# Two chunks of the FFN in one pass for a single tile, and fewer paired passes in layer 0

## The chip, the cores and the metric

The kernel runs on 1 core of one Trainium2 chip. The metric is the device time of one execution in microseconds (us), the median of several runs. The engines of the core work side by side, each on its own queue of instructions, and wait for each other through semaphores: PE (TensorE) multiplies matrices, DVE (VectorE) and ACT (ScalarE) work element by element, SP issues most of the DMAs. PE runs at a clock that a throttle grants; the profile shows the granted share, 1.00 being full speed.

## The reference

A two-layer encoder step on 1024 prompt rows and 32 sample rows, all float32. What matters here is the channel MLP (FFN) at the end of each layer, and the norms around it:

```python
for i in range(DEPTH):                       # DEPTH = 2
    mod = jax.nn.silu(c) @ w_ada[i] + b_ada[i]
    sh1, sc1, gt1, sh2, sc2, gt2 = jnp.split(mod[:, None, :], N_MOD, axis=-1)
    h = rmsnorm(x, g_norm[i, 0]) * (1 + sc1) + sh1
    ...                                      # layer 0: gating mixer, layer 1: pooling mixer
    x = x + gt1 * rmsnorm(mix, g_norm[i, 1])
    h = rmsnorm(x, g_norm[i, 2]) * (1 + sc2) + sh2
    f = jnp.square(jax.nn.relu(h @ ffn_w_up[i])) @ ffn_w_down[i]   # 1024 -> 4096 -> 1024
    x = x + gt2 * rmsnorm(f, g_norm[i, 3])
```

## The kernel before

**Tiles.** The rows are cut into three tiles of columns: tiles 0 and 1 have 384, tile 2 has 288 (256 prompt rows and the 32 sample rows). Activations lie with channels on the 128 partitions. Every float32 product is made of three matmuls in the reduced format fp32r: each operand is split into a high and a low part, and `products` (L1019) adds high by high, high by low and low by high in one PSUM bank.

**The FFN by passes.** The 4096 inner channels are cut into 8 chunks of 512. A *pass* is an entry of the list `passes` (L375 to L382): a layer, a chunk and the tiles it serves. A single-tile pass is `ffn_item` (L1448). It has four ups: each takes 24 matmuls (8 blocks of input channels, three matmuls each), then relu, square and the split into high (`fh`, on ACT) and low (`fl`, on DVE). Then its `down` makes the 8 output blocks `d`, 12 matmuls each, and `accumulate` (L1287) adds each block to `acc` in SBUF on DVE (for chunk 0 ACT copies it instead). `down` is not run at once: it goes on the list `pending`, and `flush` runs it after the first up of the next pass.

A pass for both tiles 0 and 1 is `pair_item` (L1504). It computes the ups of both tiles with seven products of blocks in place of eight (a scheme of Strassen's kind on the 2 by 2 blocks of weights and activations), 168 matmuls in place of 192, then 192 matmuls of downs. For that it needs sums and differences of the two tiles' activations, made once per layer by `combos` (L1706) into the region of tag "R", into the room of tile 2's activations, and in place over half of tile 0's. `combos` waits until tile 0's single passes are through (`singles`), and the first pair waits for it.

**The order of passes.** Layer 0: tile 0 with chunks 0, 1, 6, 7; tile 1 with 0, 1; the pairs 2 to 5; tile 1 with 6, 7; tile 2 with all eight. Layer 1: tile 0 and then tile 1 with chunks 0 to 3, the pairs 4 to 7, tile 2 with all eight.

**Weights.** Each chunk has 8 pieces of weights of 512 KB, 4 up and 4 down. They come through a stream (`w_chunk` L352 puts them in, `issue` L452 sends the DMAs on SP's queue into 3 raw buffers). ACT writes the high part (`wh`, L528), DVE the low part (`wl`, through L80). Six pairs of converted pieces fit at a time during the FFN. Between the weights the same stream carries pieces of `w_ada` (the conditioning matrix) for layer 1, which DVE multiplies out (`do_ada`, tiles `aa`); `some_ada` puts them behind chosen passes: in layer 0, 2 behind each single-tile pass with chunk 6 or 7 of tiles 0 and 1, and 6 behind each pair.

**Norms and mixers as fillers.** What follows a tile's last down (the norm of the FFN, the residual, layer 1's pooling mixer, its norm and residual, and the modulation that gives `hh` and `hl` for the next ups) is written as generators in a list `fillers`. `weave` (L800) runs after every up and every block of a down: it takes a step of the stream, and then steps of the first two fillers, as long as the planner's own count of DVE's time (`time["dve"]`) is behind its count of PE's (`time["pe"]`). Tile t's FFN cannot start before its filler `ffn0_t` or `ffn1_t` is done: `run_ffn` (L1901) finishes it there, whatever is left. Tile 2's modulation for layer 0 is put off to the last pair (`late_norm`, L1617). The program's scheduler then orders each engine's queue from this order of writing.

Of the kernel before, what the change touches and what calls it, by code (L numbers as in the profile page):

```python
# [10 lines left out]
F32R = mybir.dt.float32r  # L11
# [4 lines left out]
P = 128  # L16
# [11 lines left out]
NT = len(TILES)  # L28
# [7 lines left out]
def tile_stream_encoder_step(  # L36
# [100 lines left out]
    def ps_up(name):  # L137
        return psum.tile([P, 512], F32, tag="pu", bufs=2, name=name)
# [7 lines left out]
    def t_m(name):  # L146
        return work.tile([P, 384], F32, tag="m", bufs=3, name=name)
# [4 lines left out]
    def t_hid(kind, name, dtype=F32R):  # L152
        return work.tile([P, 384], dtype, tag="h" + kind, bufs=5, name=name)
# [88 lines left out]
    def add_w(key, ap, shape, kind="w"):  # L242
        stream.append((kind, key, ap, shape))
# [21 lines left out]
    lent = {"left": LENT, "called": False}  # L265
# [18 lines left out]
    def w_free(key):  # L284
        for i in held.pop(key):
            if i >= 0 and lent["called"]:
                lent["left"] -= 1
            else:
                slots.append(i)
# [60 lines left out]
                )  # L350

    def w_chunk(n):  # L352
        l, c, tiles = passes[n]
        for j in range(4):
            f = 4 * c + j
            add_w(
                ("up", n, j),
                ffn_w_up[l][:, f * P : (f + 1) * P].rearrange("(k p) f -> p k f", p=P),
                (8, P),
                ("one", "two")[j % 2] if tiles == PAIR else "w",  # L360
            )
        for q in range(4):
            add_w(
                ("dn", n, q),
                ffn_w_down[l][c * 512 : (c + 1) * 512, q * 256 : (q + 1) * 256].rearrange(
                    "(j p) d -> p j d", p=P
                ),
                (4, 256),
            )

    every = list(range(NT))
    PAIR = every[:2]
    passes = [(0, c, [0]) for c in (0, 1, 6, 7)]  # L375
    passes += [(0, c, [1]) for c in (0, 1)]
    passes += [(0, c, PAIR) for c in range(2, 6)]
    passes += [(0, c, [1]) for c in (6, 7)]
    passes += [(0, c, [NT - 1]) for c in range(8)]
    passes += [(1, c, [t]) for t in PAIR for c in range(4)]  # L380
    passes += [(1, c, PAIR) for c in range(4, 8)]
    passes += [(1, c, [NT - 1]) for c in range(8)]  # L382
    LEND_AT = ("up", 0, 0)

    rest = []
# [30 lines left out]
    for n in range(len(mixes)):  # L416
        w_groups(n)
        if n < 2:
            some_ada(8)
    for n, (l, c, tiles) in enumerate(passes):  # L420
        w_chunk(n)
        if tiles == PAIR:
            some_ada((6, 2)[l])
        elif l == 0 and c > 1 and len(tiles) == 1 and tiles != [NT - 1]:
            some_ada(2)
    some_ada(99)

    worder = [s[1] for s in stream if s[0] in ("w", "one", "two")]
# [272 lines left out]
    def stream_ready():  # L701
        k = state["next"]
        if k >= len(stream):
            return False
        if subs:
            return len(slots) >= subs[0][0]
        return len(slots) >= {"w": 2, "one": 3, "two": 3}.get(stream[k][0], 0)

    def stream_step():

        if not subs and stream[state["next"]][0] == "one":
            issue()
            state["next"] += 1
        k = state["next"]
        kind, key, ap, shape = stream[k]
        issue()
        run_deferred()
        if kind == "two":
            if not subs:
                quads(key[1], key[2], raws.pop(k - 1), raws.pop(k))  # L720
            subs.popleft()[1]()
            if not subs:
                state["next"] += 1
            issue()
            return
        r = raws.pop(k)
        if kind == "w":
            do_w(key, r)
        elif kind == "wide":
            do_ada(*key, r, 512)  # L730
        elif kind == "ada":
            if k < first_ada:
                do_ada_pe(*key, r)
            else:
                do_ada(*key, r, 256)
        else:
# [27 lines left out]
    def w_finish(key):  # L764
        w_free(key)
# [511 lines left out]
    pending = []  # L1277
# [43 lines left out]
    def sgu_item(p, t, mix, after):  # L1321
# [123 lines left out]
                flush()  # L1445
        pending.append(down)

    def ffn_item(p, t, after):  # L1448
        l, c, tiles = passes[p]
        last = t == tiles[-1]  # L1450
        n = ncol[t]
        hid = []

        def up(j):
            ps = ps_up(f"pf{l}_{c}_{t}_{j}")
            products(ps, n, up_terms(("up", p, j), t))
            if last:
                w_finish(("up", p, j))
            r = t_m(f"r{l}_{c}_{t}_{j}")
            act(out=r[:, :n], in_=ps[:, :n], func=AF.Relu)  # L1460
            a, b = t_hid("h", f"fh{l}_{c}_{t}_{j}"), t_hid("l", f"fl{l}_{c}_{t}_{j}")
            act(out=r[:, :n], in_=r[:, :n], func=AF.Square)
            split(a, b, r, n)
            hid.append((a, b))

        def down():
            for d in range(KB):
                ps = ps_dn(f"pg{l}_{c}_{t}_{d}")
                wh, wl = need_w(("dn", p, d // 2))
# [18 lines left out]
                if last and d % 2 == 1:  # L1488
                    w_finish(("dn", p, d // 2))
                weave(d % 2)  # L1490
# [12 lines left out]

    def pair_item(p, after, ends):  # L1504
        l, c, tiles = passes[p]
        n = ncol[0]
        hid = {t: [None] * 4 for t in tiles}
        made = [0]
# [181 lines left out]
    singles = []  # L1690
# [208 lines left out]
        fillers.append((f"ffn1_{t}", run()))  # L1899

    def run_ffn(l, after):  # L1901
        for p, (pl, c, tiles) in enumerate(passes):
            if pl != l:
                continue
            ends = [t for t in tiles if not any(q[0] == l and t in q[2] for q in passes[p + 1 :])]
            if tiles == PAIR:
                pair_item(p, after, ends)
                continue
            for t in tiles:
                if c == 0:  # L1910
                    if any(f[0] == f"ffn{l}_{t}" for f in fillers):
                        flush()
                    finish(f"ffn{l}_{t}")
                if tiles == [1] and c == 0:
                    singles.append(l)
                ffn_item(p, t, after if t in ends else None)

    run_ffn(0, to_pool)


# [154 lines left out]
```

## Time and profile before

| | us |
|---|---|
| median of 3 runs (2162.13, 2162.45, 2167.15) | 2162.45 |
| the profiled execution | 2162.36 |
| its span, first to last instruction | 2160.6 |
| ACT busy in it | 1050.2 |
| mean granted clock of PE in it | 0.992 |

The span has three parts: the gating mixer of layer 0 up to about 613 us, the FFN of layer 0 from there to about 1392 us (with the pooling mixer of layer 1 worked in beside it), and the FFN of layer 1 to about 2151 us, with 9 us of output after it. In the rows of the profile, `pf` and `pfa`, `pfb`, `pfc` are the PSUM tiles of ups (the latter three of pairs), `pg` those of downs, `pn` those of norms. A row of groups reads: line, engine, operation, output and inputs, shapes, count, then busy time in us with the mean of one in ns, then the idle time of the engine before it and what ended it. The lines from the profile stand with the prediction.

### The profile page before, as it was taken

Reading aid. Unit: us, or ns where it says so; the run is one execution under the profiler, and the core shown is the slowest. Engines: PE = TensorE matmul, PEld = TensorE weight load, DVE = VectorE, ACT = ScalarE, POOL = GpSimd, SP = SyncE. Lnnn points to the kernel's source line nnn. Section 1 sums busy time; section 2 is a strip of 40 time slices with the busy share of each in tenths; the row PEclk is TensorE's granted clock in tenths of the full one; section 3 lists DMA queues with packets and bytes.
Section 4 is the critical chain, followed back from the end, with each engine's and each line's share of the span. In section 5 each row is a group of like instructions: output and inputs, shape, how many; then the busy total and the mean of one; then the engine's idle time right before and its main releaser. Section 6 shows DMA issues by size and latency. Waiting matters only on the chain.

```text
span 2160.6 us, 33037 instructions
## 1 busy us (share of the span) xinstructions
PE 2116.0 (98%) x12930; PEld 2045.1 (95%) x12930; DVE 1580.9 (73%) x2778; ACT 1050.2 (49%) x1801; POOL 22.3 (1%) x44
## 2 busy tenths in 40 slices
PE   8999999999999999999999999799999999999998
PEld 6878999999999999999998999799999999999998
DVE  6778837567788757788886896957969765588564
ACT  5634331233455454443455666555655443455454
POOL 0000000000000000000000000000000000001100
PEclk9999999999999999999999999899999999999999
DMA  8586524353344543333474765455544322247762
GB/s 289 167 257 209 183 76 135 99 161 114 115 135 126 162 126 99 116 117 108 138 225 137 214 201 180 135 154 164 167 139 127 108 81 85 80 129 224 176 187 82
DMA packets 401904, 320.16 MB, mean 148 GB/s; under 512 B 47406, under 2 KB 365142, under 8 KB 401748
## 3 DMA queue, kind: packets, MB, share of 16 engines
q1 hardware_dynamic: 400820, 316.77, 48.2%
q8 instruction: 101, 1.65, 0.3%
q0 software_dynamic: 896, 1.28, 0.2%
q14 instruction: 55, 0.45, 0.1%
q10 hardware_dynamic: 32, 0.01, 0.0%
HBM read 287.34 MB, written 30.66 MB: 147 GB/s over the span
## 4 chain that ended last, share of the span: by engine, by line
PE 86%; DVE 6%; DMA 3%; ACT 3%; issue 1%; DVEq 0%; SPq 0%; ACTq 0%
PE pg L1025 10%; PE pg L1026 10%; PE pg L1024 10%; PE pf L1024 7%; PE pf L1025 7%; PE pf L1026 7%; PE po L1024 3%; PE po L1025 3%; PE po L1026 3%; PE pu L1024 3%; PE pu L1026 3%; PE pu L1025 3%; DMA raw<-in_w_ada_dram 2%; PE pv L1050 2%; PE pv L1052 2%; PE pv L1051 2%
## 5 line engine op out<-in xcount | busy, mean ns | idle before, releaser
L1024 PE MATMUL pg<-fh,wh_dn 128*128 128x384 f32 (+1 forms) x1344 | 431.5, 322 | 2.4 <-ACT wh_dn L528 2.4
L1026 PE MATMUL pg<-fh,wl_dn 128*128 128x384 f32 (+1 forms) x1344 | 429.1, 319 | 0.4 <-DVE wl_dn L80 0.4
L1025 PE MATMUL pg<-fl,wh_dn 128*128 128x384 f32 (+1 forms) x1344 | 429.3, 320 | 0.2 <-DVE fl L80 0.2
L1024 PE MATMUL pf<-hh,wh_up 128*128 128x384 f32 (+1 forms) x1024 | 325.6, 319 | 11.2 <-ACT hh L984 6.5
L1025 PE MATMUL pf<-hl,wh_up 128*128 128x384 f32 (+1 forms) x1024 | 324.4, 317 | 0.0
L1026 PE MATMUL pf<-hh,wl_up 128*128 128x384 f32 (+1 forms) x1024 | 323.7, 316 | 0.3 <-DVE wl_up L80 0.2
L528 ACT ACTIVATE wh_dn<-raw 128x1024 fp32r<-128x1024 f32 x160 | 169.1, 1058 | 198.6 <-PE pg L1025 126.8
L1024 PEld LDWEIGHTS pg<-fh,wh_dn 128*128 128x128 f32 x1344 | 252.5, 188 | 4.2 <-ACT wh_dn L528 2.6
L80 DVE TENSOR_TENSOR wl_dn<-raw,wh_dn 128x1024 fp32r<-128x1024 f32 x160 | 195.7, 1224 | 83.0 <-ACT wh_dn L528 76.6
L1025 PEld LDWEIGHTS pg<-fl,wh_dn 128*128 128x128 f32 x1344 | 252.7, 188 | 1.6 <-DVE fl L80 0.7
L1026 PEld LDWEIGHTS pg<-fh,wl_dn 128*128 128x128 f32 x1344 | 252.9, 188 | 0.7 <-DVE wl_dn L80 0.7
L80 DVE TENSOR_TENSOR acc<-acc,pg 128x384 f32<-128x384 f32 (+1 forms) x336 | 173.4, 518 | 72.9 <-PE pg L1026 72.6
L80 DVE SCALAR_TENSOR_TENSOR aa<-raw,csil,aa 128x512 f32<-128x512 f32 (+1 forms) x364 | 206.7, 623 | 20.9 <-DMA raw<-in_w_ada_dram 20.9
L80 DVE TENSOR_TENSOR wl_up<-raw,wh_up 128x1024 fp32r<-128x1024 f32 x128 | 156.3, 1222 | 81.7 <-ACT wh_up L528 81.5
L1024 PEld LDWEIGHTS pf<-hh,wh_up 128*128 128x128 f32 x1024 | 193.7, 190 | 14.0 <-ACT hh L984 7.6
L528 ACT ACTIVATE wh_up<-raw 128x1024 fp32r<-128x1024 f32 x128 | 135.5, 1060 | 130.0 <-PE pf L1025 78.4
L1026 PEld LDWEIGHTS pf<-hh,wl_up 128*128 128x128 f32 x1024 | 194.3, 190 | 1.0 <-DVE wl_up L80 0.9
L1025 PEld LDWEIGHTS pf<-hl,wh_up 128*128 128x128 f32 x1024 | 194.1, 190 | 0.9 <-DVE hl L80 0.7
L80 DVE TENSOR_TENSOR fl<-r,fh 128x384 fp32r<-128x384 f32 (+1 forms) x168 | 87.0, 519 | 43.1 <-ACT fh L1284 42.0
L1024 PE MATMUL po<-ush,wh_o 128*128 128x384 f32 (+1 forms) x336 | 108.0, 321 | 0.0
L1026 PE MATMUL po<-ush,wl_o 128*128 128x384 f32 (+1 forms) x336 | 107.7, 321 | 0.0
L1025 PE MATMUL po<-usl,wh_o 128*128 128x384 f32 (+1 forms) x336 | 107.7, 320 | 0.0
(387 smaller groups left out, 4254.7 us busy)
## 6 DMA issues: line engine op xcount, KB each, us to landing
raw<-in_ffn_w_up_dram SPq DMA_DIRECT2D x160, 512.0 KB, 4.0
raw<-in_ffn_w_down_dram SPq DMA_DIRECT2D x160, 512.0 KB, 3.4
raw<-in_w_ada_dram SPq DMA_DIRECT2D x92, 512.0 KB, 4.3
raw<-in_sgu_w_in_dram SPq DMA_DIRECT2D x40, 512.0 KB, 4.0
xd<-acc SPq DMA_DIRECT2D x8, 1536.0 KB, 7.8
raw<-in_sgu_w_out_dram SPq DMA_DIRECT2D x24, 512.0 KB, 3.6
xo_r<-xd SPq DMA_DIRECT2D x32, 384.0 KB, 4.0
vd<-vt SPq DMA_DIRECT2D x32, 256.0 KB, 4.5
```

The lines of the kernel that those rows point to most:

```text
L80: return op(out, *args, **kw)
L528: act(out=wh, in_=r, func=AF.Copy)
L1024: mm(ps[:, :n], wh, rh, start=i == 0, stop=False)
L1025: mm(ps[:, :n], wh, rl, start=False, stop=False)
L1026: mm(ps[:, :n], wl, rh, start=False, stop=i == last)
L1050: mm(ps[:m, :], a_h, wh[:, o : o + 512], start=k == 0, stop=False)
L1051: mm(ps[:m, :], a_h, wl[:, o : o + 512], start=False, stop=False)
L1052: mm(ps[:m, :], a_l, wh[:, o : o + 512], start=False, stop=k == KB - 1)
```

## The change

Each entry of `passes` gets a fourth number `m`. With m = 2 a single-tile pass takes two chunks at once: 8 ups, then downs of 24 matmuls for each of the 8 output blocks, in one PSUM group and with one accumulation. The down weights of such a pass come in 8 pieces of 128 output channels by 1024 inner ones in place of 2 times 4 pieces of 256 by 512. `down` runs at once after the eighth up and is not put on `pending`. The 8 hidden blocks need more room than the 5 buffers: `take_hid` lends 5 more from the region "R".

Layer 0 becomes: tile 0 with chunks 0 to 5 (three double passes), tile 1 with 0 and 1 (single), pairs 6 and 7, tile 1 with 2 to 5 (two double passes), tile 2 in four double passes. Layer 1: tile 0 with chunks 0 to 3 in two double passes, tile 1 with 0 to 3 (single), pairs 4 to 7 as before, tile 2 in four double passes. The pieces of `w_ada` in layer 0 stand 4 behind each double pass of tiles 0 and 1 and 6 behind each pair. `singles` is set after tile 1's first up and not before it.

```diff
-        l, c, tiles = passes[n]
-        for j in range(4):
+        l, c, tiles, m = passes[n]
+        for j in range(4 * m):
...
-        for q in range(4):
+        w = 256 // m
+        for q in range(4 * m):
             add_w(
                 ("dn", n, q),
-                ffn_w_down[l][c * 512 : (c + 1) * 512, q * 256 : (q + 1) * 256].rearrange(
+                ffn_w_down[l][c * 512 : (c + m) * 512, q * w : (q + 1) * w].rearrange(
                     "(j p) d -> p j d", p=P
                 ),
-                (4, 256),
+                (4 * m, w),
             )
...
-    passes = [(0, c, [0]) for c in (0, 1, 6, 7)]
-    passes += [(0, c, [1]) for c in (0, 1)]
-    passes += [(0, c, PAIR) for c in range(2, 6)]
-    passes += [(0, c, [1]) for c in (6, 7)]
-    passes += [(0, c, [NT - 1]) for c in range(8)]
-    passes += [(1, c, [t]) for t in PAIR for c in range(4)]
-    passes += [(1, c, PAIR) for c in range(4, 8)]
-    passes += [(1, c, [NT - 1]) for c in range(8)]
+    passes = [(0, c, [0], 2) for c in (0, 2, 4)]
+    passes += [(0, c, [1], 1) for c in (0, 1)]
+    passes += [(0, c, PAIR, 1) for c in (6, 7)]
+    passes += [(0, c, [1], 2) for c in (2, 4)]
+    passes += [(0, c, [NT - 1], 2) for c in (0, 2, 4, 6)]
+    passes += [(1, c, [0], 2) for c in (0, 2)]
+    passes += [(1, c, [1], 1) for c in range(4)]
+    passes += [(1, c, PAIR, 1) for c in range(4, 8)]
+    passes += [(1, c, [NT - 1], 2) for c in (0, 2, 4, 6)]
...
-        elif l == 0 and c > 1 and len(tiles) == 1 and tiles != [NT - 1]:
-            some_ada(2)
+        elif l == 0 and tiles != [NT - 1] and m > 1:
+            some_ada(4)
...
+    more_hid = [None, 0]
+
+    def take_hid(name, many):
+        if not many:
+            more_hid[:] = [None, 0]
+        else:
+            i = more_hid[1]
+            more_hid[1] += 1
+            if i % 10 >= 5:
+                if more_hid[0] is None:
+                    assert not lent["left"]
+                    more_hid[0] = work.tile([P, 5, 2, 384], F32R, tag="R", bufs=1, name="fx" + name)
+                return more_hid[0][:, i % 5, 0], more_hid[0][:, i % 5, 1]
+        return t_hid("h", "fh" + name), t_hid("l", "fl" + name)
...
-                for j in range(4):
-                    o = j * 256 + (d % 2) * P
+                for j in range(4 * m):
+                    o = j * 256 // m + (d % 2) * P * (2 - m)
...
-        for j in range(4):
+        for j in range(4 * m):
             up(j)
             weave()
             if j == 0:
                 flush()
-                if l == 1 and c == 7 and last and t == NT - 1:
+                if tiles == [1] and c == 0:
+                    singles.append(l)
+                if l == 1 and c + m == 8 and last and t == NT - 1:
                     load_last()
-        pending.append(down)
+        if m > 1:
+            down()
+        else:
+            pending.append(down)
```

More of the change, by code (lines that the diff above doesn't have):

```diff
@@ L419, in tile_stream_encoder_step @@
             some_ada(8)
-    for n, (l, c, tiles) in enumerate(passes):
+    for n, (l, c, tiles, m) in enumerate(passes):
         w_chunk(n)
@@ L1446, in sgu_item @@
         pending.append(down)
+    more_hid = [None, 0]
[11 more added lines that the diff above has]
+        return t_hid("h", "fh" + name), t_hid("l", "fl" + name)
     def ffn_item(p, t, after):
-        l, c, tiles = passes[p]
+        l, c, tiles, m = passes[p]
         last = t == tiles[-1]
@@ L1460, in up @@
             act(out=r[:, :n], in_=ps[:, :n], func=AF.Relu)
-            a, b = t_hid("h", f"fh{l}_{c}_{t}_{j}"), t_hid("l", f"fl{l}_{c}_{t}_{j}")
+            a, b = take_hid(f"{l}_{c}_{t}_{j}", m > 1)
             act(out=r[:, :n], in_=r[:, :n], func=AF.Square)
@@ L1468, in down @@
                 ps = ps_dn(f"pg{l}_{c}_{t}_{d}")
-                wh, wl = need_w(("dn", p, d // 2))
+                wh, wl = need_w(("dn", p, d * m // 2))
                 terms = []
-                for j in range(4):
-                    o = j * 256 + (d % 2) * P
+                for j in range(4 * m):
+                    o = j * 256 // m + (d % 2) * P * (2 - m)
                     a, b = hid[j]
@@ L1487, in down @@
                             turn_last(d - 1)
-                if last and d % 2 == 1:
-                    w_finish(("dn", p, d // 2))
-                weave(d % 2)
+                if last and (d + 1) * m % 2 == 0:
+                    w_finish(("dn", p, d * m // 2))
+                weave((d + 1) * m % 2 == 0)
             if after is not None:
                 after(st)
-        for j in range(4):
+        for j in range(4 * m):
             up(j)
@@ L1498, in ffn_item @@
                 flush()
-                if l == 1 and c == 7 and last and t == NT - 1:
+                if tiles == [1] and c == 0:
+                    singles.append(l)
+                if l == 1 and c + m == 8 and last and t == NT - 1:
                     load_last()
-        pending.append(down)
+        if m > 1:
+            down()
+        else:
+            pending.append(down)
     def pair_item(p, after, ends):
-        l, c, tiles = passes[p]
+        l, c, tiles, _ = passes[p]
         n = ncol[0]
@@ L1901, in run_ffn @@
     def run_ffn(l, after):
-        for p, (pl, c, tiles) in enumerate(passes):
+        for p, (pl, c, tiles, m) in enumerate(passes):
             if pl != l:
@@ L1913, in run_ffn @@
                     finish(f"ffn{l}_{t}")
-                if tiles == [1] and c == 0:
-                    singles.append(l)
                 ffn_item(p, t, after if t in ends else None)
```

## The prediction

> **What bounds the kernel now.** I read the page first, then who waited for whom on PE, then busy times by stretches of the span.
>
> ```profile
> span 2160.6 us, 33037 instructions
> PE 2116.0 (98%) x12930; PEld 2045.1 (95%) x12930; DVE 1580.9 (73%) x2778; ACT 1050.2 (49%) x1801; POOL 22.3 (1%) x44
> ...
> PE   8999999999999999999999999799999999999998
> ...
> DVE  6778837567788757788886896957969765588564
> ...
> PEclk9999999999999999999999999899999999999999
> ```
>
> PE is busy for 98% of the span, so its matmuls set the time, except where PE sinks and its clock with it. The longest waits of PE:
>
> ```profile
> PE pn_r_0x L897 <- ACT sc_r_0x L882: 8.8, 1, 8.8
> PE pf L1024 <- ACT hh L984: 6.5, 2, 5.1
> ...
> PE pf L1024 <- ACT wh_up L528: 3.7, 2, 2.0
> PE pn_rf L897 <- ACT sc_rf L882: 2.7, 1, 2.7
> PE pg L1024 <- ACT wh_dn L528: 2.4, 1, 2.4
> PE pg L1025 <- DVE fx L80: 1.8, 6, 0.5
> ...
> PE pg L1025 <- DVE fl L80: 0.2, 1, 0.2
> ```
>
> The stretches in which these waits fall, beside undisturbed ones (columns: start:end length, busy time and instructions of each engine, granted clock, DMA share, GB/s):
>
> ```profile
> core 0: us, PE busy (x) PEld busy (x) DVE busy (x) ACT busy (x) POOL busy (x), PEclk, DMA share, GB/s
> 664.30:730.80 66.50, 66.50 (x385) 66.50 (x385) 51.04 (x80) 31.16 (x47) 0.00 (x0) 1.00 0.49 144
> 890.00:953.40 63.40, 63.15 (x369) 62.55 (x368) 50.77 (x82) 25.45 (x43) 0.00 (x0) 1.00 0.38 110
> ...
> 1188.70:1226.90 38.20, 38.20 (x290) 38.20 (x289) 31.74 (x46) 25.34 (x40) 0.00 (x0) 1.00 0.71 214
> 1164.50:1200.00 35.50, 34.59 (x260) 34.35 (x260) 17.16 (x19) 23.70 (x43) 0.00 (x0) 1.00 0.54 157
> 1296.00:1331.00 35.00, 35.00 (x266) 35.00 (x266) 20.28 (x28) 20.20 (x34) 0.00 (x0) 1.00 0.69 209
> 1363.10:1414.90 51.80, 37.93 (x222) 36.12 (x221) 49.52 (x75) 28.00 (x48) 0.00 (x0) 0.84 0.46 144
> 1132.70:1176.00 43.30, 38.04 (x231) 35.43 (x230) 33.56 (x70) 26.10 (x53) 0.00 (x0) 0.92 0.41 121
> 2041.90:2101.10 59.20, 54.47 (x386) 53.67 (x385) 33.91 (x44) 28.04 (x42) 0.00 (x0) 0.94 0.63 184
> ```
>
> The reader sees two paces, 66.5 / 385 = 0.173 us a matmul of 384 columns and 38.2 / 290 = 0.132 us one of 288, and three sore places.
>
> At **1132.7 to 1176.0** tile 2's FFN of layer 0 begins. Its 96 downs of tile 1 and 120 ups of tile 2 should take 16.6 + 15.8 us; with up to 1.5 us for 15 small norm and fold matmuls that is 33.9 of 43.3: 9.4 us lost. PE waits 2.7 us for the norm and 1.4 us (the smaller of the `hh` waits) for the modulation, and then runs at a lowered clock.
>
> At **1363.1 to 1414.9** layer 1 begins with tile 0. 96 downs of 288 columns, 120 ups of 384 and some 0.7 us of norm matmuls are 12.7 + 20.8 + 0.7 = 34.2 of 51.8 us: 17.6 lost. DVE is busy 49.52 us of it: the chain pool, residual, norm, modulation of tile 0 is late, and DVE carries it.
>
> At **2041.9 to 2101.1**, late in layer 1, 386 instructions at 0.132 make 51.0 of 59.2 us: 8.2 lost, waiting for weights converted late (`wh_up`, `wh_dn`).
>
> **The change part by part.** All sums stand against the profiled execution's own 2162.36 us (span 2160.6 plus 1.8 around it), which is the median 2162.45 to within 0.1.
>
> *Pairs.* Two paired passes of layer 0 become single ones. A pair takes 63.4 us, two single passes 66.5. By these rows two pairs cost 2 x 3.1 = 6.2 us; by the count of matmuls 2 x 24 x 0.173 = 8.3. The first is smaller since a pair's stretch also holds a fold of `w_ada` and a short wait, and the fold moves elsewhere. I take **+7**, between 6.2 and 8.3. All other matmuls keep their number.
>
> *Weights.* Layer 0 loads 22 chunks for 20, 16 pieces more, and the double passes read down weights in rows half as long.
>
> ```profile
> raw<-in_ffn_w_up_dram SPq DMA_DIRECT2D x160, 512.0 KB, 4.0
> raw<-in_ffn_w_down_dram SPq DMA_DIRECT2D x160, 512.0 KB, 3.4
> L528 ACT ACTIVATE wh_dn<-raw 128x1024 fp32r<-128x1024 f32 x160 | 169.1, 1058 | 198.6 <-PE pg L1025 126.8
> ...
> L80 DVE TENSOR_TENSOR wl_dn<-raw,wh_dn 128x1024 fp32r<-128x1024 f32 x160 | 195.7, 1224 | 83.0 <-ACT wh_dn L528 76.6 <-PE pfb L1538 6.2
> L80 DVE TENSOR_TENSOR acc<-acc,pg 128x384 f32<-128x384 f32 x224 | 123.2, 551 | 48.4 <-PE pg L1026 48.2
> L80 DVE TENSOR_TENSOR fl<-r,fh 128x384 fp32r<-128x384 f32 x104 | 57.9, 557 | 25.0 <-ACT fh L1284 24.4
> L80 DVE TENSOR_TENSOR acc<-acc,pg 128x288 f32<-128x288 f32 x112 | 50.2, 451 | 24.5 <-PE pg L1026 24.4
> ```
>
> The up pieces already have the short rows (128 numbers) and land in 4.0 us, the down pieces in 3.4. With 3 raw buffers a piece every (4.0 + 1.06 + 1.22) / 3 = 2.1 us can pass, where 24 matmuls take 4.15 or 3.17 us. Cost nothing; three loads in flight and the stock of converted pieces cover it. Without that cover it is 0.6 us for each late piece; I allow 0 to 4 us.
>
> *Accumulations.* A double pass adds to `acc` 8 times, not 16. With chunk 0 left to ACT, 384-column additions fall from 224 to 168, those of 288 from 112 to 48: 56 x 0.551 + 64 x 0.451 = 60 us less of DVE. That is off PE's path and counts only where DVE is late, below.
>
> *Start of tile 2 and of layer 1.* Between the last pair and tile 2, tile 1 now has four chunks to go, before two. A chunk of 33.2 us asks of DVE 8 x 1.22 for weights, 4 x 0.557 for `fl` and 4 x 0.551 for `acc`, 14.2 us, and two pieces of `w_ada`. These (and, in the last row, `combos`) are priced by
>
> ```profile
> L80 DVE SCALAR_TENSOR_TENSOR aa<-raw,csil,aa 128x512 f32<-128x512 f32 x196 | 138.0, 748 | 16.7 <-DMA raw<-in_w_ada_dram 16.6
> ...
> L80 DVE TENSOR_SCALAR aa<-raw,csil 128x512 f32<-128x512 f32 x28 | 12.7, 483 | 10.1 <-DMA raw<-in_w_ada_dram 10.1
> ...
> L80 DVE TENSOR_TENSOR combo_z<-hh,hl 128x768 f32<-128x768 f32 x8 | 7.7, 956 | 0.0
> ```
>
> as 4 operations for each of 56 pieces, 150.7 / 56 = 2.7 us, and on average one more, a transpose or a reduction of about 0.7: some 3.4 us a piece. So 12 us of DVE are left over per chunk, 24 for the two. In tile 2's passes 32 accumulations fewer leave 14 us more, and the stream's reordering (12 pieces of `w_ada` behind tile 0's passes for 4) takes 8 x 3.4 = 27 us of DVE out of the stretch from the pairs on. Against this stand 9.4 and 17.6 us of PE lost to chains that DVE carries. Supply exceeds demand, but both tiles' chains share it, and the planner hands it out. Bounds: all 27 us come back, or none. I take **-7** at tile 2's start and **-15** at layer 1's. What is late next is tile 1's chain in layer 1; the same order as before, with more slack.
>
> The price of a wait here includes the clock: granted 0.92 over 43.3 us is 3.5 us lost, with no single wait over 2.7 us. The Trainium skill ("TensorE: Matmul & The Clock Gate", Part 1) has the half clock follow an idle window of about 3.4 us; by that rule these 3.5 us would not be lost and the recovery would be 6, not 9.4. The trace shows them, so the row decides.
>
> *The joint.* `down` right after the eighth up adds a wait: PE's 22nd matmul of the down needs the eighth `fh`, the 23rd the eighth `fl`. Behind it on PE stands everything, and DVE's next accumulation waits for that.
>
> ```profile
> L1284 ACT ACTIVATE fh<-r 128x384 fp32r<-128x384 f32 x104 | 54.0, 520 | 1.9
> L1462 ACT ACTIVATE r<-r 128x384 f32<-128x384 f32 x64 | 33.4, 521 | 1.3
> L1460 ACT ACTIVATE r<-pf 128x384 f32<-128x384 f32 x64 | 30.2, 472 | 1.1 <-PE pf L1026 1.0
> ```
>
> The chain is 0.47 + 0.52 + 0.52 + 0.56 = 2.1 us and some starts; 21 matmuls cover 3.6 us, or 2.8 with 288 columns, where the chain is shorter too. It holds unless a converted weight (1.06 on ACT, 1.22 on DVE) or a filler stands in front. The nearest row is the pair, whose downs also follow at once, behind 24 matmuls of cover: its waits for `fx` are 1.8 us in 8 passes. There are 15 double passes. Bounds 0 and 1.5 us each; I take 0.2, **+3**.
>
> *`combos`* can start later, since "R" is in use until tile 0's last down, but two single passes (66 us) remain for what is 16 operations of 0.96 and 16 of the size of `fl`, 0.56, some 24 us of DVE. Cost nothing, up to 5 if DVE is not free. `take_hid`'s buffers are read only by earlier downs, done by then: nothing.
>
> *Late layer 1.* 24 stores of outputs stand on SP's queue ahead of weights there. Down weights used in the order in which they are loaded make the stock last a little longer. I take **-2** of the 8.2, bounds -8 and +4.
>
> Sum: 2162.4 + 7 - 7 - 15 + 3 - 2 = 2148. The chain at the end (transposes, store) is unchanged.
>
> **The rivals.**
>
> *A, slower: it is the order and not the amount of DVE's work.* In 1164.5 to 1200.0 DVE is busy only 17.16 us of 35.5, in 1296.0 to 1331.0 only 20.28 of 35, while tile 0's chain was still open. The planner counted DVE as taken (a forced finish puts its clock far ahead), or a buffer was. If that governs, slack brings nothing: both waits stay, and 2162.4 + 7 + 3 = 2172. It decides once less than 10 us of the 27 come back. Against it: the first of these pauses follows the forced finish of tile 2's chain, which would itself go, and at layer 1's start DVE is truly full.
>
> *B, one of two.* Tile 2's start is cured, the chain of tile 0 stays late by half, as tile 1's pool takes its share: 2148 + 7.5 = 2155.5, on the edge of what can be told. For it: the forced finish works on the first two fillers together.
>
> *C, the joints.* 1.5 us each, as where DVE runs behind: 2148 - 3 + 22 = 2167. Against it: the 0.2 us of PE's wait for `fl`, though with 24 more matmuls of cover.
>
> **How the numbers follow.** A change under 0.3% (6.5 us) cannot be told from none here. Forecast 0.54, own range 2134 to 2155; A 0.24; B 0.16, half of it faster and half the same; C 0.06, a third each faster (half as dear), the same and slower. Faster: 0.54 + 0.08 + 0.02 = 0.64; same: 0.08 + 0.02 = 0.10; slower: 0.24 + 0.02 = 0.26. The range takes in the full recovery at both places (-5) with the bound of the late layer (-6) and no joints (-3), 2134, and a margin of two for the pairs' lower price, 2132; above it reaches to A with a little over the upper price of the pairs, 2175.
>
> **What would show it.** Right: in the profile after, the waits `pn_r_0x <- sc_r_0x` and `pf <- hh` shrink from 15.3 us together to under 4, no stretch at tile 2's or layer 1's start has a clock under 0.95, 168 and 48 accumulations stand in the groups, PE has some 48 matmuls more, and `pg <- fl` or `fx` stays under 5 us. Wrong: the two starts lose over 17 us still (A), or the waits of `pg` for `fl`, `fx`, `fh` pass 15 us (C), or weights (`wh_dn`, `wl_dn`) hold PE for more than 10.

## The result, and the profile after

The changed kernel takes 2146.89 us (median of 4 runs, 2144.05 to 2147.74). The kernel before took 2162.61 beside it (4 runs, 2162.13 to 2167.15). The medians differ by 15.7 us or 0.7%; the ratio over all runs is 0.992, 95% interval 0.9903 to 0.9938. The forecast was 2148. The profiled execution took 2147.74 us, with a span of 2145.7 and a mean granted clock of 0.997, before 0.992.

The page of after, span and busy times:

```profile
span 2145.7 us, 33068 instructions
...
PE 2116.0 (99%) x12978; PEld 2049.7 (96%) x12978; DVE 1527.3 (71%) x2638; ACT 1051.6 (49%) x1793; POOL 22.3 (1%) x44
```

PE has the 48 matmuls more, some 48 x 0.173 = 8.3 us of work, and yet the same 2116.0 us of busy time. The better clock pays for a part: PE is busy at half clock for 17.3 us before and 7.4 after, which is worth some 5 us. Where the other 3 went was not traced. The gain in the span is idle time of PE, 2160.6 - 2116.0 = 44.6 us before and 29.7 after. The waits of PE after:

```profile
PE pg L1024 <- ACT fh L1284: 5.9, 3, 5.2
...
PE pf L1024 <- ACT wh_up L528: 2.4, 1, 2.4
PE pg L1024 <- ACT fx L1284: 2.0, 3, 1.1
...
PE pg L1025 <- DVE fx L80: 1.1, 3, 0.5
...
PE pf L1026 <- DVE wl_up L80: 0.9, 2, 0.7
...
PE pg L1025 <- DVE fl L80: 0.2, 1, 0.2
```

The waits for `sc_r_0x`, `sc_rf` and `hh` at the two starts (8.8 + 2.7 + 6.5 = 18.0 us) are gone from the list. At its top stands a new one: a product of a down waiting for a hidden block, the joint of the double pass. The stretches of after (columns as before): a double pass of tile 0, a pair, tile 1's last downs with tile 2's first ups, tile 2's first downs, the start of layer 1 with the downs ahead of it, and the late stretch in layer 1.

```profile
760.50:827.10 66.60, 66.60 (x392) 66.31 (x391) 40.74 (x54) 28.60 (x41) 0.00 (x0) 1.00 0.54 159
956.60:1019.50 62.90, 62.90 (x370) 62.52 (x368) 48.58 (x78) 28.40 (x50) 0.00 (x0) 1.00 0.43 128
1120.60:1180.60 60.00, 59.90 (x396) 59.46 (x395) 54.16 (x87) 32.42 (x55) 0.00 (x0) 1.00 0.55 161
1180.60:1213.20 32.60, 27.35 (x195) 27.12 (x194) 18.11 (x21) 14.33 (x23) 0.00 (x0) 0.90 0.68 199
1356.10:1425.20 69.10, 69.10 (x421) 64.89 (x419) 44.95 (x73) 42.36 (x72) 0.00 (x0) 1.00 0.61 181
2025.40:2082.80 57.40, 53.70 (x386) 52.58 (x385) 33.21 (x38) 29.46 (x44) 0.00 (x0) 0.97 0.63 179
```

In the third and the fifth row, where the two starts lie, PE is busy all but 0.1 us, at full clock. Tile 2's norm (`pn_r_2x`) now stands on PE at 1053.0, 101 us ahead of tile 2's first up; before it stood at 1150.3, 6 us ahead. The fourth row is the new loss: 192 matmuls of 288 columns want 25.3 us and take 32.6. Two short timelines (start, length in us, engine, line, operation) show how. First ACT, then PE:

```profile
1182.22 1.04 ACT L528 ACTIVATE wh_dn<-raw 128x1024 fp32r<-128x1024 f32 x1
1186.43 1.06 ACT L528 ACTIVATE wh_dn<-raw 128x1024 fp32r<-128x1024 f32 x1 [3.16 <-DMA raw<-in_ffn_w_down_dram]
1187.39 0.39 ACT L1476 ACTIVATE r<-pf 128x288 f32<-128x288 f32 x1
1187.82 0.44 ACT L1478 ACTIVATE r<-r 128x288 f32<-128x288 f32 x1
1188.29 0.44 ACT L1284 ACTIVATE fh<-r 128x288 fp32r<-128x288 f32 x1
```

```profile
1183.24 0.29 PE L1026 MATMUL pg<-fh,wl_dn 128*128 128x288 f32 x1
1188.79 0.61 PE L1024 MATMUL pg<-fh,wh_dn 128*128 128x288 f32 x1 [5.25 <-ACT fh L1284]
1189.19 0.45 PE L1024 MATMUL pg<-fx,wh_dn 128*128 128x288 f32 x1
```

The relu of the eighth up stands on ACT's queue behind the conversion of a down weight whose load has not landed. ACT is idle 3.16 us, then converts, then makes the block, and PE waits 5.25 us. The loads and accumulations after:

```profile
raw<-in_ffn_w_up_dram SPq DMA_DIRECT2D x168, 512.0 KB, 4.0
raw<-in_ffn_w_down_dram SPq DMA_DIRECT2D x168, 512.0 KB, 3.9
```

```profile
L80 DVE TENSOR_TENSOR acc<-acc,pg 128x384 f32<-128x384 f32 x168 | 91.8, 547 | 58.0 <-PE pg L1026 57.8
L80 DVE TENSOR_TENSOR acc<-acc,pg 128x288 f32<-128x288 f32 x48 | 21.7, 452 | 39.0 <-PE pg L1026 38.9
```

Accumulations are the 168 and 48 forecast. Down pieces, 120 of 168 now with the short rows, land in 3.9 us in place of 3.4 (medians).

### The profile page after: what moved, and what is told of

It reads as the page before. It is cut to its first block, busy times and chain, and to the rows that moved or that the text cites. A ratio compares the mean times of both kernels' runs of the same rounds, so it can differ in the third digit from the quotient of the medians.

```text
span 2145.7 us, 33068 instructions
## 1 busy us (share of the span) xinstructions
PE 2116.0 (99%) x12978; PEld 2049.7 (96%) x12978; DVE 1527.3 (71%) x2638; ACT 1051.6 (49%) x1793; POOL 22.3 (1%) x44
## 4 chain that ended last, share of the span: by engine, by line
PE 85%; DVE 6%; DMA 4%; ACT 3%; issue 1%; SPq 0%; DVEq 0%; ACTq 0%
PE pg L1025 10%; PE pg L1024 10%; PE pg L1026 10%; PE pf L1024 7%; PE pf L1026 7%; PE pf L1025 7%; PE po L1025 3%; PE po L1026 3%; PE po L1024 3%; PE pu L1024 2%; PE pu L1026 2%; PE pu L1025 2%; PE pv L1050 2%; PE pv L1052 2%; PE pv L1051 2%; DMA raw<-in_w_ada_dram 2%
## 5 line engine op out<-in xcount | busy, mean ns | idle before, releaser
L1024 PE MATMUL pg<-fh,wh_dn 128*128 128x384 f32 (+1 forms) x952 | 309.2, 325 | 5.9 <-ACT fh L1284 5.9
L1025 PE MATMUL pg<-fl,wh_dn 128*128 128x384 f32 (+1 forms) x952 | 308.6, 324 | 0.2 <-DVE fl L80 0.2
L1026 PE MATMUL pg<-fh,wl_dn 128*128 128x384 f32 (+1 forms) x952 | 308.1, 324 | 0.0
L80 DVE SCALAR_TENSOR_TENSOR aa<-raw,csil,aa 128x512 f32<-128x512 f32 (+1 forms) x364 | 205.0, 618 | 13.9 <-DMA raw<-in_w_ada_dram 13.8
L1024 PE MATMUL pg<-fx,wh_dn 128*128 128x384 f32 (+1 forms) x584 | 187.2, 321 | 2.0 <-ACT fx L1284 2.0
L1025 PE MATMUL pg<-fx,wh_dn 128*128 128x384 f32 (+1 forms) x584 | 186.6, 320 | 1.2 <-DVE fx L80 1.1
L1026 PE MATMUL pg<-fx,wl_dn 128*128 128x384 f32 (+1 forms) x584 | 185.6, 318 | 0.0
L1024 PEld LDWEIGHTS pg<-fh,wh_dn 128*128 128x128 f32 x952 | 178.9, 188 | 6.8 <-ACT fh L1284 6.6
L80 DVE TENSOR_TENSOR acc<-acc,pg 128x384 f32<-128x384 f32 (+1 forms) x216 | 113.5, 526 | 97.1 <-PE pg L1026 96.8
L1025 PEld LDWEIGHTS pg<-fl,wh_dn 128*128 128x128 f32 x952 | 179.0, 188 | 1.1 <-DVE fl L80 0.9
L1026 PEld LDWEIGHTS pg<-fh,wl_dn 128*128 128x128 f32 x952 | 178.9, 188 | 0.0
L1025 PEld LDWEIGHTS pg<-fx,wh_dn 128*128 128x128 f32 x584 | 110.2, 189 | 3.4 <-DVE fx L80 2.8
```

The source lines that it names most:

```text
L80: return op(out, *args, **kw)
L1024: mm(ps[:, :n], wh, rh, start=i == 0, stop=False)
L1025: mm(ps[:, :n], wh, rl, start=False, stop=False)
L1026: mm(ps[:, :n], wl, rh, start=False, stop=i == last)
```

## The experiments

The question was which of the three reliefs that the prediction counted together (accumulations saved, two more chunks of tile 1 behind the pairs, `w_ada` moved to tile 0's passes) cured the two starts, whether it was their amount of work, and what the pairs and the joints cost. Ratios are to the kernel before, timed beside each run on the same chip, with 95% intervals; beside these runs it took some 2166 us, not 2162.6, so compare runs by their ratios. "The starts" are two places: in the kernel before, PE waits at tile 2's start in layer 0 for `pn_rf` (2.7 us) and `hh` (1.4), and at layer 1's start for `pn_r_0x` (8.8) and `hh` (5.1).

**x1_order: the order alone.** The kernel before, single passes throughout, with the changed kernel's order and places of `w_ada`.

```diff
-    passes = [(0, c, [0]) for c in (0, 1, 6, 7)]
+    passes = [(0, c, [0]) for c in range(6)]
...
-    passes += [(0, c, PAIR) for c in range(2, 6)]
-    passes += [(0, c, [1]) for c in (6, 7)]
+    passes += [(0, c, PAIR) for c in (6, 7)]
+    passes += [(0, c, [1]) for c in range(2, 6)]
...
-        elif l == 0 and c > 1 and len(tiles) == 1 and tiles != [NT - 1]:
+        elif l == 0 and (tiles == [0] or tiles == [1] and c > 1):
             some_ada(2)
```

> The order of passes and the places of w_ada of the changed kernel, with single passes throughout and downs put off as before. Theory (the two late starts were cured by the longer way to them and by w_ada moved forward): both waits for the norms go, 2162.6 + 7 for the two pairs - 9 - 17 = about 2144 to 2150, and no joint to pay. Rival (the fewer accumulations of double passes cured them): the starts of tile 2 and of layer 1 still lose over 15 us together, 2158 or more.

2149.36 us, 0.9924 (0.9905 to 0.9943). No wait for the starts is left, with every accumulation in place. The order with its places of `w_ada` suffices, and brings as much as the whole change.

**x2_double: double passes, four pairs.** The changed kernel with the four pairs of before and before's places of `w_ada`.

```diff
-    passes = [(0, c, [0], 2) for c in (0, 2, 4)]
+    passes = [(0, c, [0], 2) for c in (0, 6)]
...
-    passes += [(0, c, PAIR, 1) for c in (6, 7)]
-    passes += [(0, c, [1], 2) for c in (2, 4)]
+    passes += [(0, c, PAIR, 1) for c in range(2, 6)]
+    passes += [(0, c, [1], 2) for c in (6,)]
...
-        elif l == 0 and tiles != [NT - 1] and m > 1:
+        elif l == 0 and tiles != [NT - 1] and m > 1 and c == 6:
             some_ada(4)
```

> Double passes wherever single-tile passes come in twos, but the four pairs of layer 0 (chunks 2 to 5) and the places of w_ada of the kernel before. Theory (length of way): only tile 2's 14 us fewer accumulations help; tile 2's start loses its 9 us as before, layer 1's start some 5 of 17, 13 joints cost 5 to 9: 2152 to 2160. Rival (accumulations): both starts are cured and the two pairs kept: about 2147 - 7 = 2140.

2140.76 us, 0.9888 (0.987 to 0.9905). Again no wait for the starts. So the double passes suffice too, without the order, and the two effects do not add. Against the changed kernel it is 0.32% or 7 us better. That is near the price of two pairs, but the two kernels also differ by two double passes and in the places of `w_ada`. x1_order and x9_ada_only (below), also two pairs apart, differ by 0.2% or 4 us.

**x3_ada_back: `w_ada` back behind the pairs.** The changed kernel with 10 pieces behind each pair and 4 at tile 0.

```diff
-            some_ada((6, 2)[l])
-        elif l == 0 and tiles != [NT - 1] and m > 1:
+            some_ada((10, 2)[l])
+        elif l == 0 and m > 1 and (tiles == [1] or tiles == [0] and c == 4):
```

> The changed kernel with 8 pieces of w_ada put back from tile 0's passes to behind the two pairs (10 each in place of 6): 27 us of DVE work return to the stretch between the pairs and layer 1. Theory (DVE's slack decides): some of the late starts come back, 5 to 12 us more than the changed kernel, 2152 to 2159. Rival (the longer way alone has slack enough): within 3 us of the changed kernel, 2144 to 2150.

2167.4 us, 1.0007 (0.9997 to 1.0016). Both theories missed. The starts stay cured, and what they had brought is lost in another place. Who waited on PE, and the last pair and the passage behind it by stretches (ups, downs, tile 1's next ups):

```profile
PE pf L1024 <- ACT wh_up L528: 11.0, 2, 8.6
...
PE ada L644 <- DVE part L630: 3.6, 2, 2.0
```

```profile
957.80:991.90 34.10, 30.19 (x169) 29.14 (x170) 26.50 (x37) 20.58 (x35) 0.00 (x0) 1.00 0.44 133
991.90:1034.80 42.90, 34.30 (x201) 33.23 (x200) 42.20 (x76) 9.47 (x19) 0.00 (x0) 0.95 0.48 143
1034.80:1072.40 37.60, 36.00 (x200) 35.06 (x201) 26.89 (x34) 25.12 (x38) 0.00 (x0) 0.92 0.86 264
```

SP's queue there, in order of time:

```profile
993.25 20.76 SPq L476 DMA_DIRECT2D raw<-in_w_ada_dram  x5
...
1029.71 0.38 SPq L476 DMA_DIRECT2D raw<-in_ffn_w_up_dram  x1
```

The pieces of `w_ada` stand ahead of the next up weights in the one stream. Five of them take 20.76 us to go out; DVE, which must work them off before a raw buffer comes free, is busy 42.20 of 42.90 us. The next up weight is not even asked for before 1029.71.

**x4_deferred: the joint.** The changed kernel, with the down of a double pass put off behind the first up of a following double pass, whose weights the stream brings first (`later(n)`: this pass and the next are double).

```diff
+        ups(n, range(1 if n > 0 and later(n - 1) else 0, 4 * m))
+        if later(n):
+            ups(n + 1, [0])
...
-        if m > 1:
+        if m > 1 and not later(p):
             down()
```

> The changed kernel, but where a double pass follows a double pass, its down runs after the first up of the next one, and the stream brings that up's weights ahead of the down's. Theory (the joint, with relu waiting on ACT behind a weight conversion, is what was lost at 1183 us): the waits of pg for fh, fl, fx fall from 9.2 to under 3 us and the clock drop there goes, 8 to 11 us faster than the changed kernel, 2136 to 2140. Rival (weights are late there and only the name of the wait changes): 2145 to 2149, with PE waiting for wh_dn or wh_up instead.

2142.68 us, 0.9888 (0.9869 to 0.9906). PE's waits of `pg` for `fh`, `fx`, `fl` fall from 9.2 to 3.9 us. At tile 2's start PE now waits 2.1 us for `part` and 0.6 for `wl_up` in place of the 5.25, and 6.8 us of half clock follow all the same: theory and rival each hold in part. By the ratios the kernel is 0.32%, some 7 us, faster than the changed one, where the theory had 8 to 11; the two intervals just overlap.

**x7_two_groups and x11_after_two_groups: accumulations.** In x2_double and in the changed kernel, each down block of a double pass is made in two groups of 12 products with two accumulations, so that none is saved.

```diff
-                for j in range(4 * m):
+                for h in range(m):
+                    if h > 0:
+                        ps = ps_dn(f"pg{l}_{c + 1}_{t}_{d}")
...
+                    for j in range(4 * h, 4 * h + 4):
...
-                products(ps, n, terms)
-                accumulate(t, d, ps, c == 0)
+                    products(ps, n, terms)
+                    accumulate(t, d, ps, c == 0 and h == 0)
```

> The kernel with four pairs and double passes, but each double pass's down block is done in two groups of 12 products with two accumulations, so that the vector engine has as many accumulations as with single passes; the order of passes and loads stays. Theory that the starts of tile 2 and of layer 1 are cured by fewer accumulations ahead of them: the first products of tile 2 and of layer 1 are late again by 5 to 9 us each, waits for pn_r_0x or hh of over 3 us return, ratio 0.993 to 0.996. Rival: what cures them is that the pass's downs are done before the next up starts and the loads come in that order, whatever the count of accumulations: 0.988 to 0.990, no wait for pn_r_0x or hh over 2 us.

> The changed kernel, with each double pass's down block in two groups of 12 products and two accumulations, so that the vector engine adds as often as with single passes. Theory that with two pairs the order alone gives the vector engine time enough (as in the order run, 0.9924): both starts stay cured, the accumulations that were saved are worth nothing here, ratio 0.991 to 0.994. Rival that the double passes hold their downs directly behind their ups and so need the saved accumulations, as was seen with four pairs, where the same edit cost 1.25%: waits for pn_r_0x or hh of 4 to 9 us return, ratio 0.997 to 1.002.

With four pairs: 2168.51 us, 1.0013 (1.0004 to 1.0023), where x2_double had 0.9888. PE's waits in x7_two_groups:

```profile
PE pf L1024 <- ACT hh L984: 11.0, 2, 6.2
PE pf L1024 <- ACT wh_up L528: 6.4, 2, 4.0
PE pn_r_0x L897 <- ACT sc_r_0x L882: 5.3, 1, 5.3
```

The loss is larger than the 0.993 to 0.996 expected. The places of these waits matter. Layer 1's start is late again: the 5.3 us for `pn_r_0x` and 4.8 of those for `hh`. The other 6.2 us for `hh` are at tile 1's first up in layer 1, where the kernel before does not wait. Tile 2's start in layer 0 waits for neither its norm nor `hh`, only for weights (4.0 us for `wh_up`, 1.4 for `wl_up`), and its norm runs as early as in x2_double (1115.5):

```profile
1117.18 0.29 PE L897 MATMUL pn_r_2x<-sc_r_2x,ones 128*128 128x288 f32 x1
1546.76 1.01 PE L1024 MATMUL pf<-hh,wh_up 128*128 128x384 f32 x2 [6.23 <-ACT hh L984]
```

In the changed kernel, the same edit gives 2149.07 us, 0.9919 (0.9902 to 0.9935), and no wait for the starts. So where `w_ada` has its old places, the saved accumulations are needed for layer 1's start; tile 2's chain is early without them, as the rival had it, and by what else was not separated. Where `w_ada` has been moved they are worth nothing.

**x8_tile2_double: double passes for tile 2 alone,** in both layers, else as before.

```diff
-    passes += [(0, c, [NT - 1]) for c in range(8)]
+    passes += [(0, c, [NT - 1], 2) for c in (0, 2, 4, 6)]
```

> The kernel before with its order and its places of w_ada, double passes for tile 2 alone, in both layers. Theory that the accumulations of tile 2's passes, with the ones put off to its end, make layer 1's start late, and those of tile 0's and tile 1's passes make tile 2's late: layer 1's start is cured (17.6 us of loss go to under 4), tile 2's start keeps its 9.4 us of loss; ratio 0.992 to 0.995, 2145 to 2152 us. Rival: layer 1's start is late for another reason than the count of accumulations of tile 2's passes: ratio 0.997 to 1.001.

2156.62 us, 0.9959 (0.9945 to 0.9973), between the two forecasts. PE still waits 3.8 us for `pn_r_0x`, 2.7 for `pn_rf` and 5.3 for `hh`, 11.8 of 18.0. At tile 2's start nothing has changed for these (2.7 + 1.7 us), as the theory had it; at layer 1's start 7.4 us are left of 13.9: double passes of tile 2 do part of the cure there, not all.

**x9_ada_only: the places of `w_ada` alone.** The kernel before and its passes, with 8 of 32 pieces taken from the pairs to tile 0.

```diff
-            some_ada((6, 2)[l])
-        elif l == 0 and c > 1 and len(tiles) == 1 and tiles != [NT - 1]:
+            some_ada((4, 2)[l])
+        elif l == 0 and tiles == [0]:
+            some_ada(3)
+        elif l == 0 and c > 1 and tiles == [1]:
             some_ada(2)
```

> The kernel before with its passes, and only the pieces of w_ada moved: 3 behind each of tile 0's four passes, 4 behind each of the four pairs, 2 behind each of tile 1's last two (before: 4 at tile 0's, 6 behind each pair, 4 at tile 1's). Theory that the order run was cured by work taken from the vector engine ahead of tile 2's start, of which the moved pieces are half: tile 2's start is cured without any other order (pn_r_2x's chain early, waits for hh under 1 us), about 7 us gained there, layer 1's start stays as it was (waits for pn_r_0x of 5 to 9 us), ratio 0.995 to 0.998. Rival that the number of single passes between the last pair and tile 2 is what counts: both starts stay late, ratio 0.998 to 1.002.

2145.6 us, 0.9904 (0.9889 to 0.9918), better than either expected: both starts are cured (0.2 us of wait for `hh`, none for `pn_r_0x`). These few pieces bring by themselves what the whole change brings. What they take away is seen from the first pair on, before and in x9_ada_only:

```profile
850.00:1040.00 190.00, 189.41 (x1099) 188.03 (x1098) 153.99 (x243) 78.43 (x133) 0.00 (x0) 1.00 0.38 117
```

```profile
850.00:1040.00 190.00, 189.34 (x1100) 188.16 (x1099) 136.99 (x215) 78.66 (x134) 0.00 (x0) 1.00 0.33 101
```

DVE works 17 us less in these 190 us, by 28 operations.

**x10_order_ada_back: the two more chunks alone.** x1_order with `w_ada` put back: 10 behind each of the two pairs, 8 at tile 1's last four passes, 4 at tile 0's last two, so that 28 pieces come from the first pair on, as before.

```diff
-            some_ada((6, 2)[l])
-        elif l == 0 and (tiles == [0] or tiles == [1] and c > 1):
+            some_ada((10, 2)[l])
+        elif l == 0 and (tiles == [0] and c > 3 or tiles == [1] and c > 1):
```

> The order run (all passes single, two pairs) with its w_ada pieces put back: 4 at tile 0's last two passes, 10 behind each of the two pairs, 8 at tile 1's last four. Theory that the four single passes of tile 1 behind the pairs give the time by which tile 2's chain comes early: no wait for hh of over 1 us at tile 2's start, but weights come late behind the pairs as when the same was done to the changed kernel, which cost 20 us there: ratio 0.998 to 1.003. Rival that the moved pieces of w_ada did it: waits for hh at tile 2's start and for pn_r_0x at layer 1's start return (4 to 9 us each): ratio over 1.003.

2219.36 us, 1.0244 (1.0229 to 1.0259). The rival: weights are late as in x3_ada_back, and the starts are worse than before.

```profile
PE pn_r_0x L897 <- ACT sc_r_0x L882: 16.5, 1, 16.5
PE pf L1024 <- ACT hh L984: 11.6, 3, 5.1
PE pf L1024 <- ACT wh_up L528: 10.9, 3, 8.9
```

With `w_ada` crowded like this, four chunks of tile 1 behind the pairs instead of two do not cure the starts. What they would do with the pieces spread as before is not shown: ten pieces behind one pair make weights late by themselves, as in x3_ada_back.

**x12_planner: the order of writing alone.** All reliefs so far change two things at once: what DVE has to do, and what the planner counts for it, by which `weave` holds fillers back. Here only the count changes. In the FFN the multiplications of a piece of `w_ada` count 0.7 of their estimate; passes, accumulations and the order of the stream are those of before. The count holds back steps of the stream as well as fillers (`stream_waits`, L743), so both are written at other times.

```diff
-        aa = ada_acc[0]
+        aa, was = ada_acc[0], time["dve"]
...
+        time["dve"] = was + (0.7 if state["used"] > wpos["up", 0, 0] else 1.0) * (time["dve"] - was)
```

> The kernel before, with its passes, its accumulations and its stream, but in the FFN the planner counts the vector engine's work for a piece of w_ada at 0.7 of its estimate, so that over the 28 pieces from the first pair on the planner holds back fillers by about as much less as if 8 pieces had gone. The engine's real work is the same. Theory that the amount of the vector engine's work is what made the two starts late: fillers written earlier only queue behind the same work, the waits for pn_r_0x and hh stay at 8 us or more together, or the weights' low parts come late in their place; ratio 0.997 to 1.005. Rival that it is the order, by the planner's own count, and not the amount: the waits for pn_r_0x and hh go to under 4 us and the time comes to that of the run with only the pieces moved, 0.990 to 0.994.

2145.32 us, 0.9903 (0.9887 to 0.992). My theory fell; the rival gave the time. The page of x12_planner, and its waits:

```profile
span 2144.5 us, 33061 instructions
...
PE 2111.4 (98%) x12930; PEld 2041.2 (95%) x12930; DVE 1579.7 (74%) x2778; ACT 1047.9 (49%) x1801; POOL 22.4 (1%) x44
```

```profile
PE pf L1024 <- ACT wh_up L528: 5.8, 4, 2.4
...
PE pf L1024 <- ACT hh L984: 1.1, 1, 1.1
```

DVE has the same 2778 instructions and 1579.7 us of work, before 1580.9. Yet no wait for `pn_r_0x` or `pn_rf` is left, and of those for `hh` 1.1 us. Where tile 2's norm stands on PE, before and in x12_planner:

```profile
1150.30 0.29 PE L897 MATMUL pn_r_2x<-sc_r_2x,ones 128*128 128x288 f32 x1
```

```profile
1125.43 0.29 PE L897 MATMUL pn_r_2x<-sc_r_2x,ones 128*128 128x288 f32 x1
```

It runs 25 us earlier. DVE's work up to there is nearly the same; before and in x12_planner:

```profile
850.00:1130.00 280.00, 277.29 (x1606) 274.62 (x1605) 229.85 (x359) 118.69 (x195) 0.00 (x0) 1.00 0.47 143
```

```profile
850.00:1130.00 280.00, 274.72 (x1587) 271.36 (x1587) 226.89 (x356) 117.22 (x195) 0.00 (x0) 1.00 0.46 139
```

Of it 81.1 and 77.6 us go to `w_ada` (tiles `aa`). The engine, idle for 50 of 280 us, had the time all along; the chains were written too late. The earlier chains cost a little elsewhere: the waits for `wh_up` and `wl_up` grow from 3.9 to 7.4 us.

**x5_best and x6_ada_forward: the best of both.** x5_best is x2_double with the put-off downs of x4_deferred. x6_ada_forward is x5_best with `w_ada` moved forward as well:

```diff
-            some_ada((6, 2)[l])
-        elif l == 0 and tiles != [NT - 1] and m > 1 and c == 6:
-            some_ada(4)
+            some_ada((4, 2)[l])
+        elif l == 0 and tiles != [NT - 1] and m > 1:
+            some_ada(6 if tiles == [0] else 4)
```

> Four pairs in layer 0 with the double passes, and the down products of a double pass put off behind the first up of the next one. Theory: what the four pairs give (0.9888 of before) and what the put-off downs give over the changed kernel (2146.9 to about 2142.7 on the scale of this case's before, 0.2%) are in different stages and add: ratio 0.985 to 0.987, about 2131 to 2135 us; the waits at the joints of the double passes (fx, fl, fh) sum to under 4 us. Rival: late weights set the pace of these stretches either way, so the put-off adds nothing to four pairs: 0.988 to 0.990, with the waits moved to wh_up and wl_up.

> The kernel with four pairs and put-off downs, with eight of the 32 w_ada pieces moved from its four pairs to tile 0's two double passes and tile 1's (6 behind each of tile 0's, 4 behind each pair, 4 behind tile 1's double at c=6). Theory that the one stream of loads is what is late at tile 2's start and in the last pairs: the waits for wh_up, wl_up and part in these stages (2 to 3 us in all in the run with put-off downs alone) go, 2 to 4 us faster than the kernel it is made from: ratio about 0.984 to 0.985. Rival: the pieces stand ahead of the next weights wherever they are put, and tile 0's doubles or the first pair get the same wait instead: no difference from the kernel it is made from, or up to 5 us slower.

x5_best: 2131.55 us (2129.26 to 2133.17), 0.9837 (0.9822 to 0.9851). It beats both kernels, by more than the 0.985 to 0.987 forecast, which took the put-off downs at 0.2% where the ratios give 0.3%. x6_ada_forward: 2132.47 us, 0.9837 (0.9815 to 0.9858), no difference, as its rival had it: once the starts are cured, moving pieces buys nothing. What is left in x5_best, behind the wait for the first rows of input that every run has (4.6 us), are short waits:

```profile
PE pg L1033 <- ACT fx L1293: 2.7, 4, 1.1
PE pg L1034 <- DVE fx L80: 2.2, 7, 0.5
PE pf L1035 <- DVE wl_up L80: 2.2, 2, 1.4
```

## Why the prediction was right, point by point

The time was right to 1.1 us, by terms of which some were off in opposite directions, and with a wrong account of why the starts would be cured. That it came so near is in part luck.

- *Pairs, +7.* Right. A pair (one chunk of two tiles) takes 62.9 us after, a double pass (two chunks of one tile) 66.6: 3.7 each, 7.4 for two. The runs, in which more than the pairs differs, give 7 (0.9888 against 0.992) and 4 (0.9904 against 0.9924).
- *Weights, 0 to 4.* Right as far as PE waits for up weights (2.4 + 0.9 us). The late down weight at the joint is another matter, below.
- *Tile 2's start, -7.* Right in size: in the stretch of 60.0 us, 192 + 192 matmuls take 33.2 + 25.3 = 58.5, so at most 1.5 us are lost, before 9.4: -8. The 3.5 us that the text gave to the clock there are too many: of 6.8 us at half clock PE was busy for 5.0, which loses 2.5. The sign of no clock under 0.95 held at the starts themselves, but not in the stretch behind tile 2's (0.90), where the joint falls. *Layer 1's start, -15.* PE was idle 51.80 - 37.93 = 13.9 us there at a clock of 0.84; after, it is busy 69.10 of 69.10 us at 1.00. All 17.6 us came back, the upper bound.
- *Why: supply exceeds demand of DVE's work.* This is the step that failed. The 24 us from two more chunks did not save x10_order_ada_back, though there the crowded pieces made weights late too. The 14 us of accumulations saved are worth nothing in the changed kernel (0.9919 without them, 0.992 with), and in x7_two_groups tile 2's chain is early without them. The moved pieces, priced at 27 us, suffice (x9_ada_only), but not because DVE had too much to do: x12_planner gets the same from the count alone. Rival A named the cause, that the planner counted DVE as taken, and drew the wrong conclusion. Slack goes into the planner's count as well, so it does cure an order that the count had made. That the changed kernel too owes its cure to the count, and not to work really saved, was not tried in that kernel itself; it is an inference from x12_planner.
- *Joints, +3.* Mis-sized. `pg` waited for `fh`, `fx` and `fl` 5.9 + 2.0 + 1.1 + 0.2 = 9.2 us, before 1.8 + 0.2 and 0.9 us for `fx` on ACT, so some 6 more, and about 2 of lowered clock after the longest: +8. The text had the condition, a converted weight in front of the relu. It missed that this conversion could itself be waiting for a load (it took late weights as covered by three loads in flight and the stock), which made one joint cost 5.25 us where 0.2 each was taken. Their bound of 1.5 us each held on average.
- *`combos`, 0.* No wait in the list goes to it.
- *Late layer 1, -2.* Right in size: 386 x 0.132 = 51.0 of 57.4 us, 6.4 lost, before 8.2. That the stock lasts longer, the reason given, was not tested.

These terms, 7.4 - 8 - 17.6 + 8 - 1.8, make -12; the spans differ by 14.9. Of the 3 us more, 1.8 are a wait for `wh_up` just ahead of tile 2's start that is gone; the rest I did not trace.

## What to carry to other kernels

Where a program's order comes from a planner's count of an engine's time, change the count first: one factor brought as much here as a rewrite of the passes, and an engine with idle time ahead of a late chain (busy for only 17.16 of 35.5 us, in the prediction) is the sign to look for. A long joint is not seen from the durations of its chain; look at what stands before it on the same queue, and what that waits for. Work of low urgency in the same stream as urgent loads can cost more by its place than by its size: 8 pieces moved took all of a 0.7% gain away.

## What the runs showed of the hardware

The lowered clock has its own timing. PE's last matmul ahead of the joint ends at 1183.53; single microseconds after it:

```profile
1185.00:1186.00 1.00, 0.00 (x0) 0.00 (x0) 0.74 (x1) 0.00 (x0) 0.00 (x0) 0.96 0.82 240
1186.00:1187.00 1.00, 0.00 (x0) 0.00 (x0) 0.00 (x0) 0.57 (x1) 0.00 (x0) 0.50 0.75 224
...
1191.00:1192.00 1.00, 1.00 (x6) 1.00 (x5) 0.87 (x2) 0.51 (x2) 0.00 (x0) 0.50 1.07 325
1192.00:1193.00 1.00, 1.00 (x7) 1.00 (x6) 1.00 (x3) 0.00 (x0) 0.00 (x0) 0.62 0.97 283
1193.00:1194.00 1.00, 1.00 (x10) 1.00 (x9) 0.50 (x2) 0.00 (x0) 0.00 (x0) 1.00 0.77 268
```

The grant falls to half at about 1185.9, 2.4 us into the idle time, and comes back at about 1192.8, 4 us after the matmuls resumed at 1188.79. By the Trainium skill ("TensorE: Matmul & The Clock Gate", Part 1), activity is watched in free-running windows of about 3.4 us. The 6.8 us at half are two such windows; that the fall came after 2.4 us of idle is shorter than the one idle window of which that page speaks, and the measurement decides. In the kernel before it also came 2.4 us into a wait, that of 2.7 us for `pn_rf` (1151.08 to 1153.46), and in x4_deferred it came after a wait of only 2.06 us: the matmul ahead of it ended at 1158.59, and the half clock ran from 1160.84, with PE back at work, for 6.8 us.
